# One decoder layer on one core: HGRN outputs at fixed later places, the start reordered, eight row blocks kept for the last tiles, two projection steps ahead of HGRN's end

## The chip, the cores and the metric

One core of one Trainium2 chip. The metric is device microseconds of one execution of the whole program. TensorE (PE) does the matmuls and transposes, VectorE (DVE), ScalarE (ACT) and GpSimd (POOL) do the element work, and DMA queues, issued from SyncE (SP), ACT and POOL, move data between HBM and the on-chip memories: SBUF, where operands lie, and PSUM, into which TensorE writes.

## The reference, cut to what matters

One layer (x is 1024 positions by 1024 channels, all float32): modulated input, one input projection split ten ways, two recurrent branches, gates, an output projection, and a squared-ReLU MLP of width 4096.

```python
cond = jax.nn.silu(c)
mod = cond @ w_ada[l] + b_ada[l]
shift1, scale1, gate1, shift2, scale2, gate2 = jnp.split(mod[:, None, :], 6, axis=-1)
u = x * (1.0 + scale1) + shift1
hq, hf, hi, hg, rq, rk, rv, rg, ga, gb = jnp.split(u @ w_in[l], split_at, axis=-1)
ya = _hgrn2(hq, hf, hi, hg, lower_bounds[l]) @ w_pa[l]       # 8 heads of 128
yb = _retention(rq, rk, rv, rg, positions) @ w_pb[l]         # 4 heads, q and k rotated, v 512 wide
y = (jax.nn.sigmoid(ga) * ya + jax.nn.sigmoid(gb) * yb) @ w_o[l]
x = _layer_norm(DEEPNORM_ALPHA * x + (1.0 + gate1) * y, ln1_g[l], ln1_b[l])
u = x * (1.0 + scale2) + shift2
h = jnp.square(jax.nn.relu(u @ w_up[l] + b_up[l]))
y = h @ w_down[l] + b_down[l]
x = _layer_norm(DEEPNORM_ALPHA * x + (1.0 + gate2) * y, ln2_g[l], ln2_b[l])
```

HGRN is a gated linear recurrence: the state is scaled by a forget gate at every position, and each output is normed over its head, then multiplied by a gate (`hg`).

## The kernel before, in words

**Dense products.** A float32 product is made of three matmuls of rounded operands (`mm3`, lines 186 to 188): high by high, low by high, high by low. The parts come from `split`: ACT copies the rounded value (L181), DVE subtracts it (L182). Large projections are done as block products with seven in place of eight (`seven`, `seven_rows`, `down_seven`).

**Order.** A tile framework with a scheduler decides in which order the instructions stand on each engine; dependences become semaphores. An instruction given to `keep_in_program_order` is not moved by it. Tiles come from pools with a fixed number of buffers, so a load waits until the last reader of its buffer is done; where one pool replaces another, the first user of the new one waits for the old one's readers.

**Start, to about 75 us.** `ada(gi)` makes, group by group, the columns of scale1 and shift1: for each of eight row blocks of `w_ada` (tiles `adw`), DVE multiplies by the condition and adds (`ada_step`, L595 and L597), then TensorE sums over partitions (L603) and DVE forms `mod` (L605). The sums of both sections go side by side. `columns()` transposes the rows of biases and norms (tile `rows`, tiles `cols`, L574 and L575); `forget_bound()` makes the lower bound of the forget gates. Meanwhile x comes as `xg` (8 loads of 512 KB), is transposed (L662) and becomes the input blocks `U`, and the first gate products run. A mask of float32 is loaded on ACT's queue (L637) and cast to `mask8` on POOL; only HGRN reads it. At step k = 3 POOL's queue writes the block sum B12 (tile `U`, L690, 1024 KB) to `b12_d`.

**Block products, to about 790 us.** `seven` runs over a list of units, each one 256-column piece of a projection with an own end: `use_gate` (a sigmoid on ACT, and for `hg` a product on DVE, then a store) or `use_turned` (the rotation of rq or rk, six DVE operations L739 to L744 for each half, two stores). The list `kept` of the last twelve ends with the key unit ("rk", 3).

**Gate columns and RetNet head 0, 780 to 880 us.** `gate_proj` (L932, L933) uses new pools; `r_head(0)` loads rq and rk again (tiles `e`, L1026) and transposes the keys on TensorE (L1038); L1072 and L1074 load and scale its values, L1104 begins its products.

**HGRN, 880 to 1260 us.** Four pairs of heads (`h_pair_rec`, p = 0 to 3), each head by `h_rec`. It builds a score matrix S by levels. Level 1 (L814): two matmuls for each of four PSUM banks `psa`, then two predicated copies (L817, L818) through the mask into S. Levels 2, 8 and 32 (`H_SIZES`): two matmuls a bank (L850), three predicated copies (L857), then products that prepare the next level (L839 to L842 and L860 to L863, tiles `U`, `fk`, `D`). After the levels comes the recurrence, four steps for each half: L873 turns the keys, L884 and L885 the output in `psc`, L890 the state's update, ACT copies the output and squares it (L886, L887). Then POOL takes the power (L900), ACT scales four blocks (L902), and `h_out` is put off by `H_DEFER` steps (6, for the last pair 8, counted by `tick`): it transposes the four blocks (L910), multiplies by the gate (L912) and stores. Between the steps `weave` (a fixed proportion) and, at the end, `mix` (positions on a common axis) put dense work: `h_fill`, then the RetNet output projection `pb` (`r_first`, its evictions L1212) and `r_head(1)`.

**To the end.** RetNet heads, merge, output projection, norm, MLP. `down_seven` keeps the last `DOWN_TAIL` row blocks ("parts") of its last product back, and does them tile by tile: for each of four tiles all kept parts (18 matmuls with six), then on DVE the chain of the last residual and norm (`first_part` L1461 to L1465, `second_part` L1237 to L1472), and stores.

## Time and profile before

| what | value |
|---|---|
| median of 3 runs | 2311.68 us (2309.23 to 2312.78) |
| profiled execution | 2314.34 us |
| its span in the trace | 2312.5 us |
| mean granted TensorE clock | 0.994 |

The page puts the granted clock and the DMA share in forty equal slices of 57.8 us:

```profile
PEclk9999999999999999999999999999999999999999
DMA  9676755533333442121224756865235444877763
```

A digit is a tenth; 9 is nine tenths or more. The first slice has a DMA share of nine tenths, and so is the start. In rows of operations a name like L182 is a line of the kernel before; in the rows of the changed kernel the same statements stand at other lines: L186 to L188 are L184 to L186 there, L814 is L811, L850 is L847, L873 to L890 are L878 to L895, L902 is L911, L910 is L920, and L1038 is L1050.

### The profile page before, as it was taken

What the parts mean: (1) busy time and instruction counts of PE and PEld (TensorE: products, weight loads), DVE (VectorE), ACT (ScalarE), POOL (GpSimd) and SP (SyncE); (2) the same over time, 40 slices, a digit from 0 to 9 for tenths busy, and PEclk for the clock granted to TensorE, in tenths of its full rate; (3) what the DMA queues carried; (4) which work ended last, traced back from release to release, by engine and by line L of the source; (5) the groups of instructions that cost most, each with busy time, mean ns of one, the idle gap of its engine ahead of it and who ended that gap; (6) DMA issues with size and microseconds to landing.
All of it is one profiled execution on the core that took longest, in us unless ns stands there. A gap on an engine that the chain in (4) does not pass through costs nothing.

```text
span 2312.5 us, 29901 instructions
## 1 busy us (share of the span) xinstructions
PE 2251.2 (97%) x10366; PEld 1852.5 (80%) x10366; DVE 1653.2 (71%) x3078; ACT 1007.8 (44%) x1829; POOL 294.6 (13%) x460
## 2 busy tenths in 40 slices
PE   6999999999999999999989999999999999999998
PEld 4888888888888788878877788888878888888886
DVE  7866768686777465778876667668786666667778
ACT  3533334544333362333435555222565555644441
POOL 0111111111111020010011222013112111100001
PEclk9999999999999999999999999999999999999999
DMA  9676755533333442121224756865235444877763
GB/s 273 206 235 227 239 185 184 174 125 103 111 113 114 164 146 87 42 87 55 78 96 142 263 178 211 281 221 178 90 128 183 154 152 152 282 263 243 258 216 111
DMA packets 227416, 390.07 MB, mean 169 GB/s; under 512 B 17480, under 2 KB 122688, under 8 KB 226496
## 3 DMA queue, kind: packets, MB, share of 16 engines
q1 hardware_dynamic: 197232, 290.15, 39.1%
q0 software_dynamic: 29712, 97.55, 11.3%
q8 instruction: 82, 1.34, 0.2%
q14 instruction: 70, 0.57, 0.1%
q10 hardware_dynamic: 320, 0.45, 0.1%
HBM read 286.36 MB, written 101.72 MB: 168 GB/s over the span
## 4 chain that ended last, share of the span: by engine, by line
PE 76%; issue 11%; DVE 5%; DMA 4%; ACT 2%; POOL 1%; SPq 0%; ACTq 0%; DVEq 0%; POOLq 0%
PE psd L187 14%; PE psd L188 14%; PE psd L186 14%; PE psa L187 4%; PE psa L186 4%; PE psa L188 4%; PE psc L187 3%; PE psc L186 3%; PE psc L188 3%; PE psb L1118 2%; PE psb L186 1%; PE psb L188 1%; PE psb L187 1%; PE psc L1104 1%; DMA onr<-or_d 1%
## 5 line engine op out<-in xcount | busy, mean ns | idle before, releaser
L186 PE MATMUL psd<-U,wh 128*128 128x512 f32 x760 | 306.2, 405 | 1.8 <-ACT wh L181 0.8
L187 PE MATMUL psd<-U,wh 128*128 128x512 f32 x760 | 305.0, 401 | 1.6 <-DVE U L182 1.6
L188 PE MATMUL psd<-U,wl 128*128 128x512 f32 x760 | 303.6, 400 | 0.0
L181 ACT ACTIVATE bh<-s 128x512 fp32r<-128x512 f32 x204 | 128.2, 633 | 245.4 <-PE psd L187 59.5
L186 PE MATMUL psd<-U,bh 128*128 128x512 f32 x496 | 193.5, 390 | 1.0 <-DVE e L448 1.0
L187 PE MATMUL psd<-U,bh 128*128 128x512 f32 x496 | 193.8, 391 | 0.0
L188 PE MATMUL psd<-U,bl 128*128 128x512 f32 x496 | 193.5, 390 | 0.0
L181 ACT ACTIVATE bh<-raw 128x512 fp32r<-128x512 f32 x153 | 97.2, 637 | 215.5 <-PE psd L187 85.9
L182 DVE TENSOR_TENSOR bl<-raw,bh 128x512 fp32r<-128x512 f32 x153 | 104.5, 688 | 117.2 <-ACT bh L181 117.0
L182 DVE TENSOR_TENSOR bl<-s,bh 128x512 fp32r<-128x512 f32 x204 | 138.9, 686 | 66.3 <-ACT bh L181 66.3
L186 PEld LDWEIGHTS psd<-U,wh 128*128 128x128 f32 x760 | 143.2, 189 | 32.0 <-ACT U L181 2.6
L187 PEld LDWEIGHTS psd<-U,wh 128*128 128x128 f32 x760 | 144.3, 190 | 28.4 <-DVE U L182 2.8
L188 PEld LDWEIGHTS psd<-U,wl 128*128 128x128 f32 x760 | 144.1, 190 | 27.5 <-DVE wl L182 0.4
L181 ACT ACTIVATE wh<-raw 128x512 fp32r<-128x512 f32 (+1 forms) x87 | 61.7, 730 | 197.3 <-PE psd L187 165.3
L181 ACT ACTIVATE U<-hr 128x512 fp32r<-128x512 f32 x112 | 70.5, 630 | 145.3 <-issue 80.2
L182 DVE TENSOR_TENSOR U<-hr,U 128x512 fp32r<-128x512 f32 x112 | 76.9, 686 | 51.5 <-ACT U L181 51.3
L186 PEld LDWEIGHTS psd<-U,bh 128*128 128x128 f32 x496 | 93.4, 188 | 21.2 <-DVE e L448 1.7
L187 PEld LDWEIGHTS psd<-U,bh 128*128 128x128 f32 x496 | 93.5, 188 | 19.8 <-DVE U L182 0.5
L188 PEld LDWEIGHTS psd<-U,bl 128*128 128x128 f32 x496 | 93.5, 189 | 19.4
L857 DVE COPY_PREDICATED U<-mask,psa 128x128 f32<-128x128 uint8 x288 | 78.5, 314 | 29.7 <-PE psa L850 26.5
L186 PE MATMUL psa<-U,bh 128*128 128x512 f32 x248 | 96.7, 390 | 2.6 <-ACT e L436 2.6
L188 PE MATMUL psa<-U,bl 128*128 128x512 f32 x248 | 96.5, 389 | 0.0
(432 smaller groups left out, 5597.4 us busy)
## 6 DMA issues: line engine op xcount, KB each, us to landing
raw<-in_w_in SPq DMA_DIRECT2D x146, 512.0 KB
raw<-in_w_down SPq DMA_DIRECT2D x64, 512.0 KB
raw<-in_w_ada SPq DMA_DIRECT2D x32, 512.0 KB
raw<-in_w_up SPq DMA_DIRECT2D x32, 512.0 KB
raw<-in_w_pb SPq DMA_DIRECT2D x20, 512.0 KB
adw<-in_w_ada SPq DMA_DIRECT2D x16, 512.0 KB
v_d<-e POOLq DMA_DIRECT2D x32, 256.0 KB, 4.4
rg_d<-e POOLq DMA_DIRECT2D x32, 256.0 KB, 2.6
```

The lines of the kernel that those rows point to most:

```text
L181: self.nc.scalar.activation(hi, src, AF.Copy)
L182: self.nc.vector.tensor_tensor(lo, src, hi.bitcast(F32), op=ALU.subtract)
L186: r = mm(out, wh, uh, start=start, stop=False, skip_group_check=more)
L187: mm(out, wh, ul, start=False, stop=False, skip_group_check=more)
L188: return r, mm(out, wl, uh, start=False, stop=stop, skip_group_check=more)
L857: V.copy_predicated(dst, self.mask8[:, o:o + 128].rearrange("p (b two s) -> p b two s", two=2, s=sz), src)
L1104: mm(G[e], l[:, n % 2, es], r, start=n == 0 and i == 0, stop=i == 2, skip_group_check=n > 0)
L1118: mm(po, l, r, start=i == 0, stop=i == len(pairs) - 1)
```

## The change

The mask becomes bytes, expanded ahead of the run (1344 in each of 128 rows), and is loaded as it is. `ada` finishes the scale section's sum before the shift's, in program order for the first group, with the transposed columns behind the scale's eight steps; the exponential of the forget bound is split off and goes earlier. The write of B12 goes from POOL's queue in the middle of the loads to SP's behind them. In the list of units a gate goes from the front to the end. Level 1's matmuls write their three results interleaved, so that the predicated copies write contiguous places. For the last pair, level 32 is copied by four ACT copies of 32 partitions for each bank in place of three predicated ones on DVE. The output scale is put off by two steps and the transposes to the same total of 6 or 8; the first of each is held in program order. The steps of HGRN are dealt out anew at the end, with two of `pb`'s steps ahead. Eight parts are kept for the last tiles.

```diff
-DOWN_TAIL = 6
+DOWN_TAIL = 8
...
-N_MASK = P + 64 + 3 * 192
-N_MASK8 = P + 64 + 3 * 384
+N_MASK = P + 64 + 3 * 384
...
-        self.nc.vector.tensor_copy(self.cols, pc)
+        self.tc.keep_in_program_order(nc.vector.tensor_copy(self.cols, pc))
...
-        mask = st.tile([P, N_MASK], F32, name="mask")
-        nc.scalar.dma_start(mask, i["k_mask"])
-        nc.gpsimd.tensor_copy(self.mask8[:, :P + 64], mask[:, :P + 64])
...
-            accs = [st.tile([P, nk * P], F32, tag="acc", bufs=4, name=self.uid("acc")) for _ in ws]
-            for k in range(KT):
-                for acc, (sec, w) in zip(accs, ws):
-                    self.ada_step(acc, w[:, k, :], k, k == 0)
-            if gi == 0:
-                self.columns()
-            for acc, (sec, w) in zip(accs, ws):
+            for sec, w in ws:
+                acc = st.tile([P, nk * P], F32, tag="acc", bufs=4, name=self.uid("acc"))
+                for k in range(KT):
+                    r = self.ada_step(acc, w[:, k, :], k, k == 0)
+                    if gi == 0:
+                        self.tc.keep_in_program_order(r)
+                if gi == 0 and sec == S_SCALE1:
+                    self.columns()
+                    self.forget_exp()
...
-            if k == 3:
-                nc.gpsimd.dma_start(self.b12_d, Bf["B12"].rearrange("p k t -> p (k t)"))
...
         self.forget_bound()
+        self.tc.keep_in_program_order(nc.sync.dma_start(self.b12_d, Bf["B12"].rearrange("p k t -> p (k t)")))
...
     def start_end(self, banks, combos):
         nc = self.nc
+        nc.gpsimd.dma_start(self.mask8, self.i["k_mask"])
...
-            pa = self.ps("a", (P, 384)).rearrange("p (c w b) -> p c w b", c=2, w=3)
+            pa = self.ps("a", (P, 384)).rearrange("p (c b w) -> p c b w", c=2, w=3)
...
-                nc.tensor.matmul(pa[:, c], k[:, n * P:(n + 1) * P], q[:, :, n * 64:(n + 1) * 64], start=True, stop=True)
+                nc.tensor.matmul(pa[:, c].rearrange("p b w -> p w b"), k[:, n * P:(n + 1) * P], q[:, :, n * 64:(n + 1) * 64], start=True, stop=True)
...
+                if sz == 32 and p == 3:
+                    qv = pv.rearrange("p b w r s -> p b (w r) s")
+                    for r0, dst, src in ((0, slice(1, 2), slice(0, 1)), (64, slice(3, 4), slice(2, 3)), (32, slice(2, 4), slice(1, 5, 3)),
+                                         (0, slice(2, 4), slice(3, 6, 2))):
+                        nc.scalar.activation(Sv[r0:r0 + 32, :, dst], qv[r0:r0 + 32, :, src], AF.Copy)
...
-            for c in range(4):
-                nc.scalar.activation(ob[:, c, :], ob[:, c, :], AF.Copy, scale=rs[:, c:c + 1])
-            self.later(H_DEFER[p // 3], lambda ob=ob, hf=hf, g=g: self.h_out(h, hf, ob, g))
-            yield
+            self.later(2, lambda ob=ob, rs=rs, hf=hf, g=g: self.h_scale(p, h, hf, ob, rs, g))
+            yield
+
+    def h_scale(self, p, h, hf, ob, rs, g):
+        for c in range(4):
+            r = self.nc.scalar.activation(ob[:, c, :], ob[:, c, :], AF.Copy, scale=rs[:, c:c + 1])
+            if c == 0:
+                self.tc.keep_in_program_order(r)
+        self.later(H_DEFER[p // 3] - 2, lambda: self.h_out(h, hf, ob, g))
...
-            nc.tensor.transpose(pb[:, c * P:(c + 1) * P], ob[:, c, :], self.ident)
+            r = nc.tensor.transpose(pb[:, c * P:(c + 1) * P], ob[:, c, :], self.ident)
+            if c == 0:
+                self.tc.keep_in_program_order(r)
...
-    kept = light[:4]
-    del light[:4]
+    kept = light[:3]
+    del light[:3]
     for h in range(RH):
         kept.append((("rq", h), C_RQ + 256 * h, k.use_turned(k.rq_d[h])))
-        kept.append(light.pop(0))
+        if h < RH - 1:
+            kept.append(light.pop(0))
         kept.append((("rk", h), C_RK + 256 * h, k.use_turned(k.rk_d[h])))
+    kept += light
...
-        weave(k.h_fill(begun), islice(rec, 124), 26, 124)
+        weave(k.h_fill(begun), islice(rec, 123), 26, 123)
         pb, r1 = k.r_first(), k.r_head(1)
-        mix((rec, 30, 0, 30), (pb, 16, 0, PB_END), (r1, R1_N, R1_AT, 36))
+        for _ in range(2):
+            next(pb)
+        mix((rec, 31, 0, 31), (pb, 14, 0, PB_END), (r1, R1_N, R1_AT, 36))
```

**The first HGRN output.** On ACT, after the first half of the first pair's head (tile e_7975 holds its four outputs, ms and rs the mean square and its power), before:

```order
L886 ACTIVATE e_7975<-psc_8030 128x128
L887 ACTIVATE e_7976,ms_7977<-e_7975 128x128
L886 ACTIVATE e_7975<-psc_8039 128x128
L887 ACTIVATE e_7976,ms_7977<-e_7975 128x128
L902 ACTIVATE e_7975<-e_7975,rs_8049 128x128 x4
L886 ACTIVATE e_8064<-psc_8067 128x128
L887 ACTIVATE e_8065,ms_8066<-e_8064 128x128
L787 ACTIVATE e_8101<-psd_8076 128x512
```

and now (the same outputs are e_7972):

```order
L891 ACTIVATE e_7972<-psc_8027 128x128
L892 ACTIVATE e_7973,ms_7974<-e_7972 128x128
L891 ACTIVATE e_7972<-psc_8036 128x128
L892 ACTIVATE e_7973,ms_7974<-e_7972 128x128
L911 ACTIVATE e_7972<-e_7972,rs_8046 128x128 x2
L891 ACTIVATE e_8057<-psc_8060 128x128
L911 ACTIVATE e_7972<-e_7972,rs_8046 128x128
L892 ACTIVATE e_8058,ms_8059<-e_8057 128x128
L911 ACTIVATE e_7972<-e_7972,rs_8046 128x128
L784 ACTIVATE e_8098<-psd_8073 128x512
L891 ACTIVATE e_8057<-psc_8101 128x128
```

The four scales stood together behind the last square; now copies of the next half's outputs stand among them. On TensorE, the transposes of these outputs (psb, with cst the identity) before:

```order
L884 MATMUL psc_8067<-st_8046,U_7558 128x128
L885 MATMUL psc_8067<-U_7561,U_7553 128x128
L890 MATMUL psc_8072<-U_7561,e_8062 128x128
L910 MATMUL psb_8134<-cst,e_7975 128x128
L187 MATMUL psd_8151<-U_277,wh_7776 128x512
L910 MATMUL psb_8134<-cst,e_7975 128x128 x2
L884 MATMUL psc_8104<-st_8074,U_7558 128x128
L885 MATMUL psc_8104<-U_7561,U_7553 128x128
L890 MATMUL psc_8109<-U_7561,e_8062 128x128
L910 MATMUL psb_8134<-cst,e_7975 128x128
```

and now:

```order
L895 MATMUL psc_8115<-U_7558,e_8055 128x128
L811 MATMUL psa_8176<-hq_7557,fk_7780 128x3x64
L811 MATMUL psa_8181<-hq_7557,fk_7780 128x3x64
L889 MATMUL psc_8119<-st_8117,U_7555 128x128
L890 MATMUL psc_8119<-U_7558,U_7550 128x128
L920 MATMUL psb_8127<-cst,e_7972 128x128 x4
L811 MATMUL psa_8181<-hq_7557,fk_7780 128x3x64
L811 MATMUL psa_8186<-hq_7557,fk_7780 128x3x64 x2
L184 MATMUL psd_8247<-U_6862,wh_7773 128x512
L185 MATMUL psd_8247<-U_6863,wh_7773 128x512
```

They stood one by one among the first steps of the next half's recurrence, and now stand four together behind its last step.

**The last level of the last pair's first head.** On TensorE, before (psa_10173 and psa_10179 are the last two banks of level 8; psa_10195 to psa_10213 the four banks of level 32; psd a dense product of `pb`):

```order
L187 MATMUL psd_10365<-U_10269,wh_9872 128x512
L188 MATMUL psd_10365<-U_10269,wl_9873 128x512
L850 MATMUL psa_10173<-U_7558,fk_9660 128x192 x2
L850 MATMUL psa_10179<-U_7558,fk_9660 128x192 x2
L850 MATMUL psa_10195<-U_7558,fk_9660 128x192 x2
L850 MATMUL psa_10201<-U_7558,fk_9660 128x192 x2
L850 MATMUL psa_10207<-U_7558,fk_9660 128x192 x2
L885 MATMUL psc_10235<-U_7562,U_7553 128x128
L850 MATMUL psa_10213<-U_7558,fk_9660 128x192 x2
L814 MATMUL psa_10441<-hq_7560,fk_10033 128x192 x2
L873 MATMUL psb_10225<-cst,fk_9660 128x128 x4
L814 MATMUL psa_10446<-hq_7560,fk_10033 128x192 x2
```

and now (psa_10170 and psa_10176 close level 8 further up; these are the end of the dense work behind them and the four banks of level 32):

```order
L186 MATMUL psd_10395<-U_10236,wl_10021 128x512
L184 MATMUL psd_10395<-U_10241,wh_10020 128x512
L185 MATMUL psd_10395<-U_10241,wh_10020 128x512
L186 MATMUL psd_10395<-U_10241,wl_10021 128x512
L847 MATMUL psa_10192<-U_7555,fk_9652 128x192 x2
L847 MATMUL psa_10199<-U_7555,fk_9652 128x192 x2
L847 MATMUL psa_10206<-U_7555,fk_9652 128x192 x2
L890 MATMUL psc_10294<-U_7559,U_7550 128x128
L847 MATMUL psa_10213<-U_7555,fk_9652 128x192 x2
L811 MATMUL psa_10454<-hq_7557,fk_10025 128x3x64 x2
L811 MATMUL psa_10459<-hq_7557,fk_10025 128x3x64 x2
L878 MATMUL psb_10284<-cst,fk_9652 128x128 x4
```

Between the two levels stood nothing; now 23 dense matmuls stand there, of which four are shown. The third and fourth bank, the first product of the recurrence (psc_10294) and the next head's level 1 (L811) follow at once.

**The key transposes of RetNet head 0.** On TensorE, before: the second group (e_6927 is the last of the four loads of rq and rk) stands behind 17 dense matmuls of the gate product psd_7011 that follow the first group. The rows around it:

```order
L187 MATMUL psd_7011<-U_277,wh_6871 128x512
L188 MATMUL psd_7011<-U_276,wl_6872 128x512
L186 MATMUL psd_7011<-U_276,wh_6871 128x512
L187 MATMUL psd_7011<-U_277,wh_6871 128x512
L1038 MATMUL psa_6936<-cst,e_6927 128x128
L1038 MATMUL psa_6936<-cst,e_6926 128x128
L1038 MATMUL psa_6936<-cst,e_6927 128x128
L1038 MATMUL psa_6943<-cst,e_6927 128x128
L1038 MATMUL psa_6943<-cst,e_6926 128x128
L1038 MATMUL psa_6943<-cst,e_6927 128x128
L188 MATMUL psd_7011<-U_276,wl_6872 128x512
```

and now, with e_6924 the last load:

```order
L184 MATMUL psd_7100<-U_6862,wh_6868 128x512
L185 MATMUL psd_7100<-U_6863,wh_6868 128x512
L186 MATMUL psd_7100<-U_6862,wl_6869 128x512
L184 MATMUL psd_7100<-U_6862,wh_6868 128x512
L1050 MATMUL psa_6933<-cst,e_6923 128x128
L1050 MATMUL psa_6940<-cst,e_6923 128x128
L185 MATMUL psd_7100<-U_6863,wh_6868 128x512
L186 MATMUL psd_7100<-U_6862,wl_6869 128x512
L1050 MATMUL psa_6933<-cst,e_6924 128x128
L1050 MATMUL psa_6933<-cst,e_6923 128x128
L1050 MATMUL psa_6933<-cst,e_6924 128x128
L1050 MATMUL psa_6940<-cst,e_6924 128x128
```

Both groups stand later, in the second gate product with these weights (psd_7100), and close together.

More of the change, by code (lines that the diff above doesn't have):

```diff
@@ L76, in constants @@
             c[:, K_OSC + h * 8 + n] = np.exp(float(lg[h]) * (t - 512))
-    m = np.zeros((P, N_MASK), np.float32)
+    m = np.zeros((P, N_MASK), np.uint8)
     m[:, :P] = np.eye(P, dtype=np.float32)
@@ L81, in constants @@
     for n, s in enumerate(H_SIZES):
-        o = P + 64 + 192 * n
         half, quad = j // s % 4, j // (4 * s) == r // (2 * s)
-        m[:, o:o + 64] = (half == r // s % 2 * 2) & quad
-        m[:, o + 64:o + 128] = (half == 1) & quad
-        m[:, o + 128:o + 192] = (half == 0) & quad
+        for i, f in enumerate((r // s % 2 * 2, 1, 0)):
+            o = P + 64 + 384 * n + 128 * i
+            m[:, o:o + 64] = m[:, o + 64:o + 128] = (half == f) & quad
     return c, m
@@ L549, in consts @@
             nc.scalar.dma_start(rows[r0:r0 + n, :], ap.rearrange("o (k p) -> (o k) p", p=P))
-        self.mask8 = cp.tile([P, N_MASK8], U8, name="mask8")
+        self.mask8 = cp.tile([P, N_MASK], U8, name="mask8")
         self.ident = self.cst[:, K_ID:K_ID + P]
@@ L574, in columns, with forget_exp, forget_bound @@
         nc.tensor.transpose(pc, self.rows, self.ident)
-        nc.vector.tensor_copy(self.cols, pc)
-    def forget_bound(self):
-        nc, cp = self.nc, self.cp
+        self.tc.keep_in_program_order(nc.vector.tensor_copy(self.cols, pc))
+    def forget_exp(self):
+        nc = self.nc
         l = self.cols[:, B_LB:B_LB + 8]
         e = self.small[:, 40:48]
+        self.tc.keep_in_program_order(nc.vector.tensor_tensor(e, l, l, op=ALU.subtract))
+        nc.scalar.activation(e, e, AF.Exp)
+    def forget_bound(self):
+        nc = self.nc
+        e = self.small[:, 40:48]
         r = self.small[:, 48:56]
-        nc.vector.tensor_tensor(e, l, l, op=ALU.subtract)
-        nc.scalar.activation(e, e, AF.Exp)
         nc.vector.reciprocal(r, e)
@@ L594, in ada_step @@
         if first:
-            self.nc.vector.tensor_scalar(acc, w, sc, None, op0=ALU.mult)
-        else:
-            self.nc.vector.scalar_tensor_tensor(acc, w, sc, acc, op0=ALU.mult, op1=ALU.add)
+            return self.nc.vector.tensor_scalar(acc, w, sc, None, op0=ALU.mult)
+        return self.nc.vector.scalar_tensor_tensor(acc, w, sc, acc, op0=ALU.mult, op1=ALU.add)
     def ada_cols(self, acc, sec, k0, nk, plus, pa):
@@ L635, in start @@
                 self.w_load = 4
-        mask = st.tile([P, N_MASK], F32, name="mask")
-        nc.scalar.dma_start(mask, i["k_mask"])
-        nc.gpsimd.tensor_copy(self.mask8[:, :P + 64], mask[:, :P + 64])
-        nc.gpsimd.tensor_copy(self.mask8[:, P + 64:].rearrange("p (n c r) -> p n c r", n=9, c=2),
-                              mask[:, P + 64:].rearrange("p (n r) -> p n r", n=9).unsqueeze(2).to_broadcast([P, 9, 2, 64]))
         mods = self.ps("c", (P, 16))
@@ L810, in h_rec @@
         for bk in range(4):
-            pa = self.ps("a", (P, 384)).rearrange("p (c w b) -> p c w b", c=2, w=3)
+            pa = self.ps("a", (P, 384)).rearrange("p (c b w) -> p c b w", c=2, w=3)
             for c in (0, 1):
                 n = 2 * bk + c
-                nc.tensor.matmul(pa[:, c], k[:, n * P:(n + 1) * P], q[:, :, n * 64:(n + 1) * 64], start=True, stop=True)
-            Sv = S[bk // 2][:, bk % 2 * 2:bk % 2 * 2 + 2, :].rearrange("p c (b two) -> p c two b", two=2)
-            mk = self.mask8[:, :P].rearrange("p (b two) -> p two b", two=2).unsqueeze(1).to_broadcast([P, 2, 2, 64])
-            V.copy_predicated(Sv, mk, pa[:, :, 0:2])
-            V.copy_predicated(Sv[:, :, 1], self.mask8[:, P:P + 64].unsqueeze(1).to_broadcast([P, 2, 64]), pa[:, :, 2])
+                nc.tensor.matmul(pa[:, c].rearrange("p b w -> p w b"), k[:, n * P:(n + 1) * P], q[:, :, n * 64:(n + 1) * 64], start=True, stop=True)
+            Sv = S[bk // 2][:, bk % 2 * 2:bk % 2 * 2 + 2, :].rearrange("p c (b two) -> p c b two", two=2)
+            mk = self.mask8[:, :P].rearrange("p (b two) -> p b two", two=2).unsqueeze(1).to_broadcast([P, 2, 64, 2])
+            V.copy_predicated(Sv, mk, pa[:, :, :, 0:2])
+            V.copy_predicated(Sv[:, :, :, 1], self.mask8[:, P:P + 64].unsqueeze(1).to_broadcast([P, 2, 64]), pa[:, :, :, 2])
             if bk == 1:
```

2 lines of the change are left out of this document (added).

## The prediction, made before the changed kernel had run

> **What bounds the kernel now.** I read the head of the page first, then TensorE's waits, then a table of stretches. The page says that TensorE is the bound almost everywhere:
>
> ```profile
> span 2312.5 us, 29901 instructions
> PE 2251.2 (97%) x10366; PEld 1852.5 (80%) x10366; DVE 1653.2 (71%) x3078; ACT 1007.8 (44%) x1829; POOL 294.6 (13%) x460
> ```
>
> TensorE is busy 2251.2 of 2312.5 us, and the change takes no matmul away. So whatever it can give lies in the 61.3 us in which TensorE stands still, and in busy time at a low clock. The list of what TensorE waited for (total us, times, longest us) says where the 61.3 lie:
>
> ```profile
> PE psb L910 <- ACT e L902: 6.9, 9, 1.0
> PE psc L603 <- DVE acc L597: 6.8, 3, 3.7
> PE psc L574 <- DMA rows<-in_b_up: 4.6, 1, 4.6
> PE psa L850 <- DVE U L840: 4.5, 1, 4.5
> PE psa L1038 <- DMA e<-rk_d: 3.9, 2, 3.3
> PE psd L186 <- ACT wh L181: 0.8, 1, 0.8
> ```
>
> L910 are the transposes of the HGRN outputs, L597 and L603 the modulation sums at the start, L850 the levels of the HGRN score matrix, L1038 the transposes of a RetNet head's keys. The table of stretches shows the places (busy us of each engine, then granted clock, DMA share, GB/s):
>
> ```profile
> core 0: us, PE busy (x) PEld busy (x) DVE busy (x) ACT busy (x) POOL busy (x), PEclk, DMA share, GB/s
> 13.00:59.00 46.00, 38.45 (x153) 28.87 (x152) 38.46 (x132) 20.70 (x31) 1.44 (x2) 0.89 0.95 270
> 40.00:45.00 5.00, 2.93 (x16) 2.05 (x15) 3.81 (x11) 2.65 (x5) 0.69 (x1) 1.00 1.08 348
> 50.00:55.00 5.00, 2.37 (x9) 1.69 (x8) 4.50 (x19) 0.00 (x0) 0.00 (x0) 0.75 0.88 252
> 55.00:60.00 5.00, 5.00 (x18) 4.17 (x17) 4.59 (x15) 3.41 (x5) 0.00 (x0) 0.57 0.62 174
> 65.00:75.00 10.00, 9.84 (x49) 7.91 (x48) 9.62 (x22) 6.60 (x10) 0.00 (x0) 1.00 0.01 4
> 800.00:805.00 5.00, 2.36 (x10) 1.86 (x11) 1.08 (x2) 1.09 (x2) 0.00 (x0) 0.84 0.98 336
> 805.00:810.00 5.00, 5.00 (x27) 4.39 (x26) 1.72 (x4) 1.46 (x3) 0.00 (x0) 0.82 0.19 67
> 1180.00:1190.00 10.00, 5.47 (x23) 4.75 (x22) 7.12 (x22) 0.00 (x0) 0.00 (x0) 0.83 0.00 0
> ```
>
> Two things are to be seen. From 13 to 59 the DMA engines are busy 0.95 of the time: the start is bound by loading. And behind each idle stretch the clock drops: 2.63 us idle in 50-55 is followed by 0.57 in 55-60, the stop in 800-805 by 0.82, that in 1180-1190 shows 0.83. A wait here costs itself and then some.
>
> **The start (mask, ada order, B12 write).**
>
> ```profile
> b_d<-U POOLq DMA_DIRECT2D x1, 1024.0 KB, 7.6
> mask<-in_k_mask ACTq DMA_DIRECT2D x1, 384.0 KB
> 8.56 0.29 DVE L575 COPY cols<-psc 128x128 f32<-128x128 f32 x1 [2.86 <-PE psc L574]
> ```
>
> The mask shrinks from 384 KB to 128 x 1344 bytes, 168 KB, and the 1024 KB write of B12 goes out of the loaded stretch to behind its last load (SP row 32, between raw_416 and raw_882), when 65-75 shows a DMA share of 0.01. That is 216 + 1024 KB, 1.27 MB, at the stretch's 270 GB/s 4.7 us of DMA time. What of that TensorE gets: it idles 7.6 of the 46 us there, and behind the write alone 2.07 us in 40-45 and 2.63 in 50-55, with the slow 55-60 on top (0.43 of 5.00 busy us, 2.1). So there is room for nearly all, but gates then wait for DVE, busy 38.46 of 46. I take 3.5. The copy of cols stands second on DVE and holds it 2.86 us for the row of b_up; the change puts seven more steps of the first sum ahead of it. TensorE's 3.7 us wait for those sums shortens, but the shift sum and the first weights land later anyway, so I take 1.0 of it. **Start: 4.5**, between 0 (DVE instead of DMA sets the pace) and 7.5 (4.7 with 2.1 of clock and 0.7 more). Two casts on POOL go; nothing waits for the mask before HGRN.
>
> **Kept order (ga last in place of rk).**
>
> ```profile
> 779.57 0.68 DVE L739 TENSOR_TENSOR e<-e,cos 128x512 f32<-128x512 f32 x1
> 786.18 0.68 DVE L744 TENSOR_TENSOR e<-e,e 128x512 f32<-128x512 f32 x1
> 788.00 0.54 POOL L933 DMA_DIRECT2D gb_d<-e  x1 [0.30 <-ACT e L932]
> 792.61 2.19 ACT L181 ACTIVATE wh<-raw 128x512 fp32r<-128x512 f32 x4 [3.41 <-DMA gb_d<-e]
> 802.64 0.87 PE L1038 MATMUL psa<-cst,e 128*128 128x128 f32 x6 [3.34 <-DMA e<-rk_d]
> ```
>
> The last unit before the pools change hands is a key unit: twelve rotary steps on DVE from 779.57 to 786.9, then its writes, and ACT's next weight split waits for writes until 792.61. That costs TensorE 0.8 us, delays the release of the raw buffers, and so two 512 KB loads meet the small loads of rq and rk: 3.34 us more. With a gate as last unit there is one ACT sigmoid, and a write, for each half: some 7 us of DVE leave this chain, against 4.2 us of waits. In the order after, seven more dense matmuls stand ahead of the second group of key transposes, too. Against it: all four raw loads now stand ahead of rq and rk on SP's queue, so if they are late the wait comes back. The clock behind the stop (0.16 of 5 and 0.18 of 5) is worth 1.7. **5.0** of 5.9; bounds 0 and 5.9.
>
> The Trainium skill, "TensorE: Matmul & The Clock Gate", Part 1, puts the half clock behind at least one idle window of about 3.4 us. By that rule a 3.34 us stop, or the 2.63 us in 50-55, would cost no clock, and this term would be 4.2 at most. The trace differs here: 0.82 and 0.57 follow these stops; I go by the trace.
>
> **HGRN outputs in fixed later places.**
>
> ```profile
> 941.54 1.28 ACT L902 ACTIVATE e<-e,rs 128x128 f32<-128x128 f32 x4 [1.35 <-POOL rs L900]
> 941.99 0.33 PE L910 MATMUL psb<-cst,e 128*128 128x128 f32 x1 [0.90 <-ACT e L902]
> ```
>
> In the order before, the first transpose stands directly behind the steps with whose end the scale becomes due; ACT waits 1.35 us for POOL's power, scales, and TensorE waits for ACT. In the order after, scale comes two steps later, and transposes in one group of four at their counted place, four or more steps behind the scale. The 16 groups have 9 waits of 6.9 us. The cover is the recurrence and dense matmuls between; if it failed, a wait of 1 us each would stay. **6.0**, bounds 0 and 6.9. ACT, not held by POOL, can only be earlier with its other work.
>
> **Level 1 (strided matmul output).**
>
> ```profile
> L817 DVE COPY_PREDICATED U<-mask,psa 128x256 f32<-128x256 uint8 x32 | 22.7, 742 | 7.5 <-PE psa L814 7.2
> L839 DVE TENSOR_TENSOR U<-U,D 128x256 f32<-128x256 f32 x16 | 6.7, 420 | 0.0
> L814 PE MATMUL psa<-hq,fk 128*128 128x192 f32 x128 | 26.6, 330 | 1.3 <-DVE U L818 0.8 <-DVE ms L898 0.3
> 1179.81 1.54 PE L850 MATMUL psa<-U,fk 128*128 128x192 f32 x8 [0.20 <-DVE U L857]
> ```
>
> The predicated copy gets a contiguous destination: from 742 ns to about the 420 of a 128x256 operation, 32 times, 10 us of DVE, which the waits place almost nowhere on TensorE's path. In return the matmul writes PSUM with a step of three elements. No row shows that. L850, same size and writing runs, takes as long as L814 did, so I take **0**. The upper price by DVE's strided row: 742/420, 1.77 times. Eight matmuls in 1.54 us with the last one's 0.33 are 0.172 us each; 128 of them 22 us; 0.77 of that 17 us lost. Below, 1 us gained from DVE.
>
> **Last pair, last level; two projection steps ahead.**
>
> ```profile
> 1185.88 3.89 PE L850 MATMUL psa<-U,fk 128*128 128x192 f32 x12 [4.53 <-DVE U L840]
> L857 DVE COPY_PREDICATED U<-mask,psa 128x128 f32<-128x128 uint8 x288 | 78.5, 314 | 29.7 <-PE psa L850 26.5
> L886 ACT ACTIVATE e<-psc 128x128 f32<-128x128 f32 x64 | 17.4, 272 | 17.9 <-PE psc L885 17.2
> ```
>
> Before, TensorE reaches the last level of the last pair's first head with no dense work between the levels, and waits 4.53 us for DVE, then runs at half clock (0.17 of 10, 1.7 us). In the order after, 23 dense matmuls of 0.23 us (the pitch of the tail below) stand there, some 5.2 us: the wait goes, and so does the slow clock, 6.2 together. New waits take its place: 24 copies on DVE leave, 32 short ones come on ACT, four for each bank, by L886's 272 ns for twice the elements about 0.25 each. A bank takes 1.0 us, with two banks in flight and 0.35 us of matmuls for each; the third and fourth bank of each head wait about 0.7, 2.8 for both. Behind ACT's 32 copies are queued its evictions and the copies of the recurrence, another 0.4. And the end of the stage has two projection steps less as cover. **3.0**; bounds -2 (the end uncovered) and 6.2. The steps run ahead cost nothing themselves: their matmuls are the same.
>
> **Eight kept parts.**
>
> ```profile
> 2282.93 0.69 DVE L182 TENSOR_TENSOR U<-U,U 128x512 fp32r<-128x512 f32 x1
> 2294.08 0.68 DVE L1461 TENSOR_TENSOR row<-psd,g 128x512 f32<-128x512 f32 x1
> 2299.21 0.68 DVE L1461 TENSOR_TENSOR row<-psd,g 128x512 f32<-128x512 f32 x1
> 2307.85 1.41 DVE L1472 SCALAR_TENSOR_TENSOR row<-row,stats,lb 128x512 f32<-128x512 f32 x2
> 2300.52 0.39 PE L187 MATMUL psb<-U 128*128 128x512 f32 x1
> 2300.75 0.39 PE L188 MATMUL psb<-U 128*128 128x512 f32 x1
> ```
>
> Per last tile TensorE does 6 x 3 matmuls at a pitch of 0.227 us, 4.1 us, and DVE's chain takes 5.13 (2294.08 to 2299.21): DVE falls behind and ends at 2309.26, 8.1 us after TensorE's 2301.14. With 8 x 3, 5.45 us per tile, DVE waits for TensorE, and only one chain of 5.1 and a hand-over of 0.3 stand behind it: end 2306.6. **2.6**; less if the eighth part is split late: DVE's last split ends 2283.6, and it is due at about 2301.1 - 21.8 + 4.8 = 2284.1. Bounds 0 and 2.7.
>
> **Sum.** 4.5 + 5.0 + 6.0 + 0 + 3.0 + 2.6 = 21.1. From the profiled execution's 2314.34 (1.84 outside its span) that is 2293.2; from the median 2311.68, 2290.6. The profiled one lies 1.6 above the highest of the three, so I take the middle, **2292**.
>
> **Rivals.** *Start and last level give nothing back*: DVE paces the start, and ACT's copies keep what the 4.53 gave. For it speak DVE's 38.46 of 46 and the short copies; 21.1 - 7.5 = 13.6, about 2299.5. *The clock gives more*: start whole at 7.5, last level at 6.2: 2286, or 2284 with every bound. *The strided writes slow the matmuls*: place level 1 of all eight heads; at 1.77 times 17 us are lost (2309), at three times, one access for each written element, 44 us (2336); slower than before from a factor of about 2 (22 us against 21.1). Against it: L850's runs cost nothing. *The change doesn't do what it says*: transposes wait at their new place and rq and rk behind raw; 21.1 - 11 = 10, and with half the start 2305 to 2309.
>
> **Chances.** Forecast (2287 to 2297) 0.62; first rival (2297 to 2304) 0.18; the clock 0.09; strided 0.06, mostly slower; last 0.05. A measurement tells about 0.2%, 4.6 us, from no change. Faster 0.90, same 0.05, slower 0.05. The range takes in the forecast and most of the first and second rival: 2284 to 2303.
>
> **What would show it.** Right: no wait of TensorE for the scale; no 3 us stop for rk near 800 and full clock in 800-810; no 4.5 us stop at the last level but several under 1 us for ACT's copies; the mean of the level-1 matmuls stays near 330 ns; about 5.5 us from TensorE's last matmul to DVE's end in place of 8.1; the DMA-bound start some 4 us shorter. Wrong: a longer level-1 matmul, or one large wait at the head of RetNet's second head, where two steps of cover are gone.

## The result and the profile after

The changed kernel takes 2286.82 us (median of 4 runs, 2284.68 to 2287.82) against 2310.49 for the kernel before, taken with it (4 runs, 2309.23 to 2312.78). The ratio is 0.9895, 95% interval 0.9878 to 0.9912: 20 to 28 us faster. The forecast was 2292, range 2284 to 2303, so the time lies 5 us under the forecast and inside the range. It also lies just under the forecast's own band (2287 to 2297), where the prediction had put the rival "the clock gives more" (2286, chance 0.09). The experiments show that the number was met there for another reason.

The head of the page of the changed kernel:

```profile
span 2286.0 us, 29888 instructions
PE 2239.7 (98%) x10366; PEld 1847.6 (81%) x10366; DVE 1642.2 (72%) x3054; ACT 1013.8 (44%) x1861; POOL 290.8 (13%) x458
```

The same 10366 matmuls and transposes. TensorE's busy time fell by 11.5 us, its idle time by 15.0: the busy part is time at a low clock, and waits too short to be shown apart. In each trace the granted clock switches between full and half in pieces of 3.41 us. Ahead of the last matmul the kernel before has six pieces at half speed and the changed kernel two; a piece costs at most 1.7 us (half of it), so four fewer are worth up to 6.8 us. What TensorE waits for now (total us, times, longest us):

```profile
PE psc L572 <- DMA rows<-in_b_up: 4.9, 1, 4.9
PE psc L603 <- DVE acc L597: 3.8, 2, 2.0
PE psc L889 <- ACT e L891: 2.6, 4, 0.7
PE psd L184 <- ACT e L1224: 2.2, 2, 1.7
PE psa L1050 <- DMA e<-rq_d: 1.8, 1, 1.8
PE psc L1116 <- ACT e L1086: 1.5, 2, 1.1
```

The wait for the scale (6.9 us) and that of the last pair's level 32 for DVE (4.5) are off the list. The one for the keys fell from 3.3 to 1.8. New, or longer than before, are waits of the recurrence for ACT's copies of its outputs (L889, for the copy L891) and of a dense product for its eviction (L1224). Level 32's copies on ACT are waited for by 0.6 us in all, and the head of RetNet's second head by 1.1 us (1.4 before), so the large wait that the prediction named as a sign of being wrong did not come. The stretches that answer to those shown of before:

```profile
13.00:59.00 46.00, 40.28 (x186) 31.31 (x187) 41.61 (x141) 23.37 (x34) 0.00 (x0) 0.96 1.03 290
50.00:55.00 5.00, 5.00 (x27) 3.70 (x26) 4.79 (x17) 3.44 (x5) 0.00 (x0) 1.00 0.99 293
55.00:60.00 5.00, 5.00 (x28) 4.20 (x28) 5.00 (x17) 3.67 (x5) 0.00 (x0) 1.00 1.04 384
65.00:75.00 10.00, 10.00 (x44) 7.92 (x43) 10.00 (x13) 7.62 (x13) 1.63 (x3) 1.00 0.60 182
795.00:805.00 10.00, 10.00 (x55) 8.17 (x54) 5.78 (x11) 5.88 (x12) 1.33 (x2) 1.00 0.29 96
1170.00:1190.00 20.00, 18.39 (x110) 14.91 (x109) 11.52 (x29) 13.03 (x49) 4.95 (x7) 1.00 0.19 72
```

The clock, the third number from the end, is full where 0.57, 0.82 and 0.83 stood. In the last pair it only moved, though: the piece at half speed at 1185.7 of before stands at 1223.0 now, behind other waits, and the mean clock from the 4150th to the 4500th dense matmul is 0.991 in both kernels.

Where the time went is best read by counting matmuls. Both programs issue the same 8412 matmuls of dense products, so the start of the n-th can be compared (worked out from the two traces, us):

| n-th dense matmul | before | after minus before | what lies ahead of it |
|---|---|---|---|
| 150 | 77.9 | -7.0 | the start |
| 3150 | 766.3 | -7.0 | block products |
| 3450 | 875.4 | -10.6 | change of pools, RetNet head 0 |
| 4150 | 1150.6 | -19.1 | three pairs of HGRN |
| 4500 | 1332.8 | -21.7 | last pair, RetNet head 1 |
| 5850 | 1714.5 | -22.6 | heads, merge, output projection |
| 6000 | 1752.9 | -24.7 | begin of the MLP |
| 8400 | 2298.3 | -23.5 | MLP |
| end of DVE | 2309.3 | -26.4 | tail |

The profiled execution took 2287.82, 26.5 less than that of before (2314.34), while the medians differ by 23.7. The experiments say where this difference sits. As a measure of chance: the trace of before is the longest of all fourteen at the start and at the begin of the MLP (38.4 us, others down to 34.9).

### The profile page after: what moved, and what is told of

Its sections match the earlier page's. It is cut to its first block, busy times and chain, and to the rows that moved or that the text cites. A ratio compares the mean times of both kernels' runs of the same rounds, so it can differ in the third digit from the quotient of the medians.

```text
span 2286.0 us, 29888 instructions
## 1 busy us (share of the span) xinstructions
PE 2239.7 (98%) x10366; PEld 1847.6 (81%) x10366; DVE 1642.2 (72%) x3054; ACT 1013.8 (44%) x1861; POOL 290.8 (13%) x458
## 4 chain that ended last, share of the span: by engine, by line
PE 69%; issue 17%; DVE 5%; DMA 4%; POOL 3%; ACT 2%; SPq 0%; POOLq 0%; DVEq 0%; ACTq 0%
PE psd L185 13%; PE psd L186 13%; PE psd L184 13%; PE psa L185 3%; PE psa L184 3%; PE psa L186 3%; PE psc L185 3%; PE psc L184 3%; PE psc L186 3%; PE psb L1130 2%; PE psa L847 2%; PE psb L185 1%; PE psb L186 1%; PE psb L184 1%; PE psc L1116 1%
## 5 line engine op out<-in xcount | busy, mean ns | idle before, releaser
L184 PEld LDWEIGHTS psd<-U,bh 128*128 128x128 f32 x496 | 93.1, 188 | 21.7 <-DVE e L446 2.6
L184 PE MATMUL psa<-U,bh 128*128 128x512 f32 x248 | 96.7, 390 | 1.9 <-ACT e L434 1.9
L180 DVE TENSOR_TENSOR wl<-raw,wh 128x512 fp32r<-128x512 f32 (+1 forms) x87 | 69.9, 817 | 37.6 <-ACT wh L179 35.1
L185 PE MATMUL psa<-U,bh 128*128 128x512 f32 x248 | 96.5, 389 | 0.0
```

The costliest lines, as they stand in the source:

```text
L180: self.nc.vector.tensor_tensor(lo, src, hi.bitcast(F32), op=ALU.subtract)
L184: r = mm(out, wh, uh, start=start, stop=False, skip_group_check=more)
L185: mm(out, wh, ul, start=False, stop=False, skip_group_check=more)
```

## The experiments

Each is the kernel before with one part of the change, or the changed kernel without one. Times are ratios to the kernel before on the same chip, with 95% intervals; 0.001 is 2.3 us. Where in the program a part gains was read by the n-th dense matmul, as above.

**Start: the write of B12 alone.**

```diff
-            if k == 3:
-                nc.gpsimd.dma_start(self.b12_d, ...)
+        self.tc.keep_in_program_order(nc.sync.dma_start(self.b12_d, ...))
```

> The kernel before, with the write of B12 alone moved to SP's queue behind the loads. Loads bind the start (theory): the 1024 KB leave the stretch at its 270 GB/s, 3.9 us, and the slow-clock window behind the 2.37 us wait of TensorE goes too, so the 150th dense matmul starts 3.5 to 6 us earlier (77.9 us in the trace of before). Rival, DVE sets the pace of the start: under 1.5 us. Behind the start nothing changes under either.

Measured: 0.9989 (0.9978 to 1.0000). The 150th matmul starts 4.7 us earlier than in the trace of before.

**Start: the mask alone.**

```diff
-        mask = st.tile([P, N_MASK], F32, name="mask")
-        nc.scalar.dma_start(mask, i["k_mask"])
+        nc.gpsimd.dma_start(self.mask8, self.i["k_mask"])
```

> The kernel before, with the mask alone stored as bytes and loaded as it is. Loads bind the start: 216 KB less, 0.8 us earlier at the 150th dense matmul. Rival, the gain hangs on POOL's casts or on which load is first: 0 or more than 2 us.

Measured: 0.9999 (0.9987 to 1.0012); 150th matmul 3.9 us earlier.

**Start: the order of the sums alone.**

```diff
-            for k in range(KT):
-                for acc, (sec, w) in zip(accs, ws):
+            for sec, w in ws:
+                for k in range(KT):
```

> The kernel before, with the order of the modulation sums alone changed (scale first, columns behind the eight steps, the exponential early). Theory: the first 3.7 us wait for the sums shrinks, but what lands later then sets the end of the start, so about 1 us at the 150th dense matmul. Rival, the order and not the load volume is the gain of the start: 4 us or more here. Second rival, the shift's sums now come later and TensorE waits for them: 0 or a loss.

Measured: 0.9993 (0.9982 to 1.0004); 150th matmul 4.6 us earlier.

What follows from these three was not what any theory said: three parts, each 3.9 to 4.7 us in its trace and 0.2 to 2.5 us by its ratio, with no interval clear of 1. The traces of the experiments whose start was left as it was resolve it. Their 150th matmul starts 0.3 (units), 5.0 (outputs), 3.5 (transposes held), 2.4 (ACT's copies), 1.5 (dealing), 1.8 (tail and level 1) and 4.1 us (dealing and copies) earlier than in the trace of before. The start varies by 5 us from one execution to the next, and the trace of before caught its slowest. Most of what varies is the clock. The stretch 13-70 in before and in the kernel with the outputs alone, whose starts are the same program:

```profile
13.00:70.00 57.00, 49.29 (x209) 37.89 (x208) 47.05 (x157) 26.56 (x39) 1.44 (x2) 0.91 0.84 246
```
```profile
13.00:70.00 57.00, 49.97 (x230) 38.51 (x231) 51.52 (x162) 30.59 (x45) 1.04 (x2) 0.97 0.87 246
```

Nearly the same waits, but 0.91 of the clock in the one and 0.97 in the other: 3.4 us. Against the mean of these eight starts (2.3 us earlier than the trace of before), B12 is 2.4, the mask 1.5 and the order 2.3 us earlier; each is one execution, and inside the 0 to 5.0 us of the eight, so this alone shows none of the three.

The clock sorts them further. Between 13 and 70 the eight unchanged starts have one to three pieces at half speed (mean clock 0.97, 0.94 or 0.91). With 1.7 us taken off for each piece, their 150th matmul starts at 71.2 to 73.0 us, on the mean 72.4. Counted so, the write of B12 alone has 69.8, the mask alone 72.4 and the order alone 73.3, and the three executions with the whole new start 69.2 to 69.9. By this estimate the write of B12 carries what the start gains in waits, and nothing is seen of the mask. If the order of the sums gained, it was by the clock: the four executions with it have 0, 0, 1 and 1 such pieces, the ten without it 1 to 3. So few executions don't show that it did.

**Start: the three together** (the three diffs above in one kernel).

> The kernel before with the three start edits together (mask as bytes, B12's write later, the order of the modulation sums). Profiles of programs with the same start as before differ by up to 5 us at the 150th dense matmul, so the median decides. Theory, one load-bound stretch: 4 to 5 us faster in the median, about the sum of the three alone (1.7, 0 and 1.5 us), as loads and order shorten the same chain. Rival, the 7.0 us that the trace of the changed kernel shows are all the edits': a median 6.5 us or more faster.

Measured: 0.9988 (0.9979 to 0.9997), 2.8 us with 0.7 to 4.9. Its trace shows the 150th matmul 8.5 us earlier; the three traces with the whole new start (this, the changed kernel, and the one without ACT's copies) have 8.5, 7.0 and 6.3, on the mean 7.2, against 2.3 for the eight old starts: 4.9 us. The medians themselves are 3.9 us apart. The rival of 6.5 or more falls. The start is worth 3 to 5 us, as forecast (4.5).

**The list of units alone.**

```diff
-    kept = light[:4]
+    kept = light[:3]
...
+    kept += light
```

> The kernel before, with the list of units alone changed (a gate as last in place of the last key unit). Theory: the chain of twelve rotary steps and writes ahead of the release goes, the 0.8 us wait and the 3.3 us wait of the key transposes go with the 1.7 us of clock behind them, so -4 to -6 us between the 3150th and the 3450th dense matmul. Rival: the four raw loads ahead of rq and rk on SP's queue keep the transposes waiting some 2 us, and the gain is 2.5 to 4.

Measured: 0.9980 (0.9971 to 0.9989), 4.6 us. In the trace 4.0 us lie between the 3150th and the 3450th matmul, 3.6 in the changed kernel. The eleven traces with the old list take 107.4 to 110.1 us there (mean 108.8), the three with the new one 105.1 to 105.7, so 3.4 us on the mean. All eleven have one piece at half speed between 787 and 807, and none of the three has, so this part of the clock's gain is no chance. The chain ahead of the weight split is gone, yet a wait for the loads is left, here in the changed kernel (SP's queue, where L1038 are the loads of rq and rk there; ACT; TensorE):

```profile
781.07 0.97 SPq L336 DMA_DIRECT2D raw<-in_w_in  x2
783.64 1.12 SPq L336 DMA_DIRECT2D raw<-in_w_in  x2
784.81 1.33 SPq L1038 DMA_DIRECT2D e<-rq_d  x2
786.24 1.74 SPq L1038 DMA_DIRECT2D e<-rk_d  x2
779.69 2.19 ACT L179 ACTIVATE wh<-raw 128x512 fp32r<-128x512 f32 x4 [2.65 <-DMA ga_d<-e]
794.26 0.41 PE L1050 MATMUL psa<-cst,e 128*128 128x128 f32 x2 [1.82 <-DMA e<-rq_d]
```

The split starts at 779.69 in place of 792.61, of which 7.0 us are the earlier start and 5.9 this edit. But rq and rk are issued behind 2 MB of raw weights, from 784.81 on, and the first key transposes, which wait for rq, start at 794.26. Both theories hold in part: the waits shrink and the clock stays full, and 1.8 us remain.

**The HGRN outputs alone.**

```diff
-            for c in range(4):
-                nc.scalar.activation(ob[:, c, :], ob[:, c, :], AF.Copy, scale=rs[:, c:c + 1])
-            self.later(H_DEFER[p // 3], ...h_out...)
+            self.later(2, ...h_scale...)
```

> The kernel before, with the HGRN outputs alone changed (scales two steps later, transposes held at their counted place). Theory: TensorE's 6.9 us of waits for the scale go and little comes for them, -5 to -6.5 us up to the end of HGRN. Rival, seen in the trace of the changed kernel: the scales now stand in ACT's queue among the copies of the recurrence, and TensorE waits there for the copies of psc instead, some 3 us, so that -3 to -4 is left.

**The transposes held, the scales left where they were.**

```diff
-            nc.tensor.transpose(pb[:, c * P:(c + 1) * P], ob[:, c, :], self.ident)
+            r = nc.tensor.transpose(pb[:, c * P:(c + 1) * P], ob[:, c, :], self.ident)
+            if c == 0:
+                self.tc.keep_in_program_order(r)
```

> The kernel before, with the transposes of the HGRN outputs alone held at their counted place; the scales stay together right behind the last square. If the place of the transposes is the cause, this gives as much as both parts or more (-5 to -7 us), and ACT still waits about 21 us for POOL's power. If ACT's wait for POOL is what delays TensorE, it gives clearly less than both parts together, and TensorE waits for the copies of psc behind the scales.

Measured: outputs 0.9976 (0.9965 to 0.9988), transposes held alone 0.9977 (0.9965 to 0.9989). From the 3450th to the 4150th matmul, the first three pairs of HGRN, they gain 6.5 and 6.3 us. The seven executions in which nothing was changed in this stretch agree to 0.1 us (275.0 to 275.2), so both are far outside of chance. The scale's group on ACT, before, with the transposes held, and in the changed kernel:

```profile
L902 ACT ACTIVATE e<-e,rs 128x128 f32<-128x128 f32 x64 | 20.8, 391 | 20.9 <-POOL rs L900 20.9
```
```profile
L902 ACT ACTIVATE e<-e,rs 128x128 f32<-128x128 f32 x64 | 20.8, 390 | 19.3 <-POOL rs L900 19.2
```
```profile
L911 ACT ACTIVATE e<-e,rs 128x128 f32<-128x128 f32 x64 | 21.6, 392 | 20.4 <-POOL rs L905 20.4
```

ACT waits 20 us for POOL's power in all three. In the first three pairs the place of the transposes is the whole gain; that the scales go two steps later brought nothing that can be seen there, and did not free ACT. For the last pair this stays open: from the 4150th to the 4500th matmul the trace with the transposes held alone takes 185.5 us, the one with both parts 182.9, and six executions with nothing changed there 181.9 to 183.9. The times of the two kernels are the same (medians 2305.26 and 2305.09). The rival of the first run had the waits right and the loss wrong: waits for L886, the copies of psc, appear (1.9 us at L890, 0.7 at L884), and 6.5 us are gained all the same. They appear with the scales left in place too (2.9 and 0.7), so the later scales are not their cause.

**ACT's copies alone.**

```diff
+                if sz == 32 and p == 3:
+                        nc.scalar.activation(Sv[r0:r0 + 32, :, dst], qv[r0:r0 + 32, :, src], AF.Copy)
```

> The kernel before, with the last pair's level 32 alone copied by ACT. Theory: no dense matmul comes between the levels of the pair's first head, so the 4.5 us wait for DVE stays, and the copies change little or cost: -1 to +3 us. Rival, the DVE copies were the cause of the 4.5 us wait: -3 us or better. The short copies take 0.2 to 0.3 us each.

**The dealing alone.**

```diff
-        mix((rec, 30, 0, 30), (pb, 16, 0, PB_END), (r1, R1_N, R1_AT, 36))
+        for _ in range(2):
+            next(pb)
+        mix((rec, 31, 0, 31), (pb, 14, 0, PB_END), (r1, R1_N, R1_AT, 36))
```

> The kernel before, with the dealing of the last steps alone changed (two projection steps ahead). Theory: 22 dense matmuls stand between levels 8 and 32 of the last pair's first head, the 4.5 us wait and the 1.7 us of clock behind it go, and the end of the stage loses 1 us of cover: -4 to -6 us at the 4400th dense matmul. Rival, the cover is only moved and the wait comes back at the end of the stage: -1 to +1.

**Both together** (the two diffs above).

> The kernel before with the dealing of the last steps and ACT's copies together. Alone, the dealing took the 4.5 us wait away and got a 2.5 us wait for an eviction of ACT and slow clock in 1240-1260 for it, and ACT's copies left the 4.5 us where it was. Theory, they need each other: DVE freed by the copies lets the last head's recurrence keep up, and the stretch from the 4200th to the 4500th dense matmul is 2 to 4 us shorter than before. Rival, they don't: it is 0 to 2 us longer, as with the dealing alone, and the gain of the changed kernel there comes from the later scales.

**The changed kernel without ACT's copies.**

```diff
-                if sz == 32 and p == 3:
...
-                    continue
```

> The changed kernel without ACT's copies: level 32 of the last pair by DVE as before. If the copies carry part of the gain, the stretch from the 4200th to the 4500th dense matmul is 2 us longer or more than in the changed kernel and the median lies near 2289. If they only move work (16 short copies ahead of ACT's evictions and of the recurrence's copies), it is the same or shorter, and this version is as fast as the changed kernel or faster by 1 to 2 us.

Measured, with the stretch from the 4150th to the 4500th dense matmul and TensorE's idle time in it:

| kernel | ratio | stretch, us | idle, us |
|---|---|---|---|
| before | 1 | 182.3 | 12.6 |
| copies alone | 0.9985 (0.9973 to 0.9997) | 182.1 | 11.8 |
| dealing alone | 0.9999 (0.9988 to 1.0010) | 183.6 | 14.1 |
| both | 0.9988 (0.9978 to 0.9998) | 180.6 | 13.8 |
| outputs alone | 0.9976 (0.9965 to 0.9988) | 182.9 | 12.7 |
| change without copies | 0.9925 (0.9913 to 0.9938) | 183.4 | 14.1 |
| change | 0.9895 (0.9878 to 0.9912) | 179.7 | 10.6 |

Some of TensorE's longest waits between 1135 and 1300: with the copies alone, with the dealing alone, with both, in the change without copies, and in the change. L1112 and L1108 are the first products of RetNet's second head:

```profile
PE psa L850 <- DVE U L840: 4.5, 1, 4.5
PE psc L1112 <- ACT e L1082: 3.0, 1, 3.0
```
```profile
PE psd L186 <- ACT e L1212: 2.5, 1, 2.5
PE psb L910 <- ACT e L902: 1.5, 2, 1.1
PE psa L850 <- DVE U L840: 0.7, 1, 0.7
```
```profile
PE psc L1112 <- ACT e L1082: 2.6, 1, 2.6
PE psd L186 <- ACT e L1220: 1.9, 2, 1.7
PE psa L850 <- ACT U L858: 0.7, 2, 0.4
```
```profile
PE psd L184 <- ACT e L1216: 2.5, 1, 2.5
PE psc L1108 <- ACT e L1078: 2.5, 2, 1.4
PE psa L847 <- DVE U L854: 2.3, 3, 0.9
```
```profile
PE psd L184 <- ACT e L1224: 2.2, 2, 1.7
PE psc L889 <- ACT e L892: 0.8, 2, 0.5
```

How far this stretch moves by chance: in six executions with nothing changed in it (before, the list of units, and the four of the start) it takes 181.9 to 183.9 us, with one or two pieces at half speed.

The copies alone leave the 4.5 us wait where it was, so DVE's predicated copies were not its cause. The dealing alone removes it (0.7 is left), and a dense product then waits 2.5 us for its eviction at the end of the stage, where the last head stands uncovered. TensorE idles 1.5 us longer than before and the time is the same (0.9999), so the rival of that run holds: the cover was only moved. With both, the 4.5 us wait is gone too and the stage is 1.7 us shorter, under the 2 to 4 that were expected. But TensorE idles 1.2 us longer there than before; what this execution has fewer is pieces at half speed, none against one. Its ratio is that of the copies alone (0.9988 and 0.9985). So this run does not show that the two need each other.

What is shown is the part of the copies inside the changed kernel. Without them its stretch is 3.7 us longer, 3.5 of them idle time of TensorE, with one piece at half speed in either execution. The times of the change with and without them don't overlap (2284.68 to 2287.82 and 2291.09 to 2293.18, taken on two occasions; medians 5.2 us apart), as was expected if the copies carry part of the gain. The changed kernel without the dealing was not run, so whether the copies need the dealing, or the held transposes, stays open. The time of the copies alone is open too (3.5 us, interval 0.7 to 6.2, where -1 to +3 us of change were expected): behind the start its trace gains more than 0.9 us only at the begin of the MLP (3.1), where the trace of before was slow by chance. The short copies take 268 ns for 32x128 and 208 for 32x64.

**The tail and level 1.**

```diff
-DOWN_TAIL = 6
+DOWN_TAIL = 8
...
-                nc.tensor.matmul(pa[:, c], ...)
+                nc.tensor.matmul(pa[:, c].rearrange("p b w -> p w b"), ...)
```

> The kernel before with eight kept parts and with the strided level 1, two edits at places far apart. Tail: from TensorE's last matmul to DVE's end 5.4 us in place of 8.1, but TensorE up to 0.9 us later there since the last parts are split late, so 1.8 to 2.7 us. Level 1: matmuls at 330 ns as before, predicated copies at about 450 ns in place of 742, and HGRN 0 to 1 us shorter up to its last pair. Rival, strided writes cost: the matmuls above 400 ns, HGRN 3 us longer or more. Rival for the tail: the last parts hold TensorE for 2.5 us and nothing is left.

Measured: 0.9969 (0.9958 to 0.9980), 7.2 us. The tail gives 2.9 us, from the 8400th matmul to DVE's end, and TensorE is not late. Level 1 gives 3.0 us between the 3450th and the 4150th matmul, where unchanged executions agree to 0.1 us; 0 to 1 were expected. Its groups, TensorE's and DVE's:

```profile
L814 PE MATMUL psa<-hq,fk 128*128 128x192 f32 x128 | 26.2, 330 | 0.1
L817 DVE COPY_PREDICATED U<-mask,psa 128x256 f32<-128x256 uint8 x32 | 13.9, 448 | 8.6 <-PE psa L814 8.4
```

The strided write costs TensorE nothing: 330 ns as before. The copy falls from 742 to 448 ns, and that is on TensorE's path after all.

## Why the prediction was right, and where its terms were off

| term | forecast, us | measured, us |
|---|---|---|
| start | 4.5 | 4.9 by traces, 2.8 (0.7 to 4.9) by the ratio |
| kept order | 5.0 | 4.0 alone, 3.6 in the change |
| outputs | 6.0 | 6.5 alone, first three pairs |
| level 1 | 0 | 3.0 alone, first three pairs |
| outputs and level 1 | 6.0 | 8.5 in the change, first three pairs |
| last pair | 3.0 | 2.6 in the change |
| tail | 2.6 | 2.9 alone, 2.0 in the change |

The sum was 21.1; the medians give 23.7, and the table's measured terms, by traces and as far as possible in the change, 4.9 + 3.6 + 8.5 + 2.6 + 2.0 = 21.6. The 2.1 us between 23.7 and 21.6 lie inside the interval (20 to 28). The change beat the forecast's 21.1 mainly by level 1, to which the forecast gave nothing, and not as the rival of the clock had it: the start gave 4.9 and not 7.5, the last pair 2.6 and not 6.2. That the sum came out so near is in part luck, as level 1 made up for what kept order lacked, and the last pair's term was met by other steps than those forecast.

*Start.* Right in size. Of the reason, only the write of B12 (1024 KB of the 1.27 MB) is seen to pay; for the mask and for the shorter chain of sums no gain in waits is shown. Quoting one trace for the clock was a risk not seen: the 0.57 in 55-60 comes from 6.8 us at half speed from 52.5 on. Of the eight executions with this start two have that, three have one piece of 3.4 us there, and three none.

*Kept order.* The chain and the clock went as argued, the clock in all three traces with the new list. The cover argued from the order (seven dense matmuls more) was too little: the rival, rq and rk behind raw, kept 1.8 us.

*Outputs.* The gain was right, and one step of its reason wrong: "ACT, not held by POOL, can only be earlier". ACT is held about as long as before (20.4 us, 20.9 before). That two steps of the counter are too short a distance on ACT, with little of its work between them, is argued and was not tried.

*Level 1.* The mis-sized term: the step "10 us of DVE, which the waits place almost nowhere on TensorE's path". The list showed 0.8 and 0.3 us of waits for these copies. In the run 1.8 us of TensorE's idle time went between the 3450th and the 4150th matmul, from 7.4 to 5.6 (0.7 of these waits and 0.8 of those for the scale), and 1.2 us more in the pitch of busy matmuls, which no list of waits shows; what sets that pitch stays open.

*Last pair.* The size is right, the steps are not, and that they add up is luck. The 4.5 us wait went for the reason given (23 dense matmuls). The 1.7 us of clock did not: a piece at half speed stands at 1223.0 in place of 1185.7. The 2.8 us for the third and fourth bank did not come either: waits for the copies are 0.6 us. In their place stand 2.2 us for an eviction on ACT, and TensorE's idle time in the stretch fell by 2.0 us. The copies, counted as a cost, are worth 3.7 us inside the change.

*Tail.* Right: between the last matmul and DVE's end lie 5.3 us where 8.1 were. In the changed kernel's trace (times on DVE) each tile waits for TensorE, as forecast:

```profile
2272.19 0.69 DVE L1473 TENSOR_TENSOR row<-psd,g 128x512 f32<-128x512 f32 x1 [0.21 <-PE psd L186]
2277.63 0.69 DVE L1473 TENSOR_TENSOR row<-psb,g 128x512 f32<-128x512 f32 x1 [0.21 <-PE psb L186]
2281.45 1.41 DVE L1484 SCALAR_TENSOR_TENSOR row<-row,stats,lb 128x512 f32<-128x512 f32 x2
```

There TensorE came 0.9 us late, as the last splits ended only at 2260.5, 5.7 us after the tail had begun: the margin that the forecast had at about half a microsecond was used up. In the run of the tail alone, and in the change without the copies, it was not.

*What the forecast had no term for.* 2.1 of the 26.4 us between the two traces lie at the begin of the MLP, which the change does not touch: before has a piece at half speed there and the changed kernel none. It is chance, as the last section shows.

## What to carry to other kernels

Moving cover to an early wait can give it all back at the place that it is taken from (the dealing alone: 0.9999). And an edit can be worth little alone and more inside the whole change (the copies: 0.2 us of the stretch alone, 3.7 in the change), so measure each part both ways. A transpose or any reader that a scheduler hoists to the first moment its model calls free is worth pinning at a counted distance; where the producer stood mattered less here. And before a term is read from one trace, look how that stretch differs between executions of the same code: here the start's 5 us of scatter was as large as the term. Counting the pieces at half speed in each trace tells most of that scatter.

## What the runs showed of the hardware

The same stop of TensorE costs its clock in one execution and not in the next, by where it falls in a fixed grid of 3.41 us. At the begin of the MLP (1650-1760) three kernels have the same code: the kernel before waits 2.30 us there, the one with the outputs alone 2.02, the one with the mask alone 1.82:

```profile
1650.00:1760.00 110.00, 107.06 (x480) 87.90 (x479) 90.62 (x125) 68.91 (x117) 15.86 (x29) 0.98 0.41 137
```
```profile
1650.00:1760.00 110.00, 107.30 (x484) 88.13 (x483) 92.62 (x127) 70.85 (x118) 18.03 (x33) 1.00 0.42 143
```
```profile
1650.00:1760.00 110.00, 107.58 (x482) 88.34 (x481) 91.43 (x128) 70.92 (x121) 15.83 (x29) 0.98 0.41 139
```

The longest and the shortest stop are each followed by one piece of 3.41 us at half clock, at most 1.7 of the 110 us, the middle one by none, so the length alone does not decide. In every trace the switches of the clock lie whole multiples of 3.41 us apart. On that grid the 2.30 us lie inside one piece (1714.78 to 1718.19; TensorE busy 0.33 of it) and so do the 1.82 us (1709.60 to 1713.01; 0.47); the 2.02 us are cut by the border at 1704.51, and the two pieces are busy 0.63 and 0.76. Counted over all fourteen traces, up to the last switch of each, this is what follows a piece at full clock:

| busy share of TensorE in the piece | pieces | followed by half clock |
|---|---|---|
| under 0.40 | 41 | 41 |
| 0.40 to 0.55 | 33 | 18 |
| 0.55 and more | 9194 | 2 |

So a stop of about 2 us can cost up to 1.7 us more, and whether it does is a matter of where it falls. The Trainium skill, "TensorE: Matmul & The Clock Gate", Part 1, says that the clock's windows run free of the program; that agrees with these rows, as the grid stands elsewhere against the program in each execution. The same part of the Trainium skill puts the half clock behind at least one idle window of some 3.4 us; a window without any work was not needed here, since 0.33 and 0.47 of busy time were followed by it.

A matmul written to PSUM with a step of three elements took no longer than one written in a run (330 ns both), while a predicated copy of 256 columns into places of step two took 742 ns against 448 into a run. The order in which the mask is read changed with it. But the second copy (L818), whose mask lies in a run and whose 128 places lie at step two in both kernels, took 453 and 447 ns, as long as 256 places in a run, whatever the step of its source; so the places are the likelier cause.
